# Moving a decay stage under a convolution, and pairing and deferring steps of a 16-chunk loop, in a two-layer hybrid encoder

## The chip, the cores and the metric

The kernel runs on the 8 cores of one Trainium2 chip. Each core computes one element of a batch of 8; nothing is exchanged between cores. The metric is device time in microseconds of the slowest core. Most runs of one kernel agree within 0.3%, but a program on all 8 cores has a second, slower state in some of its runs: one die, or both, shows a lower granted clock and a longer time.

The engines are called as in the profile: PE (matrix), ACT (activation functions), DVE and POOL (vector work), SP (issues transfers). PEld is weight loading on PE.

## The reference, cut to what matters

Two layers; each adds to x the output projection of three branches. The change touches only the state-space (SSD) branch:

```python
def _ssd_branch(u, conv_w, conv_b, a_log, dt_bias, d_skip, norm_w):
    z, xbc, dt = ...                                  # cuts of u
    xbc = silu(_dwconv_centred(xbc, conv_w, conv_b))  # 5 taps
    xs, bm, cm = ...                                  # cuts of xbc
    dt = softplus(dt + dt_bias)                       # two directions x 16 heads
    dta = dt * -exp(a_log)
    y_f = _ssd_chunked(xs * dt[:, :, 0], dta[:, :, 0], bm, cm)
    y_b = flip(_ssd_chunked(flip(xs * dt[:, :, 1]), flip(dta[:, :, 1]), flip(bm), flip(cm)))
    y = y_f + y_b + (d_skip[0] + d_skip[1]) * xs
    y = y * silu(z)                                   # the gate
    return y * rsqrt(mean(y * y, per group) + EPS) * norm_w
```

`_ssd_chunked` works on chunks of 128 positions: it needs the running sum of `dta` within each chunk and, inside a chunk, the products exp(-(difference of running sums)) x scores. With 2048 positions there are 16 chunks; heads come in two groups of 8.

## The kernel before

Each layer does, in the SSD part: a **decay stage** (dt, running sums `cs`, their exponentials, and `cs` transposed and written to memory as `csT_d`); then for each of two groups the convolution, a pass A over the chunk states, and **pass B**, a loop of 16 chunks. Pass B therefore runs four times. `P.op(engine, instruction, reads, writes)` puts an instruction in that engine's queue, in program order; each engine runs its queue in order, and the helper adds the waits that the reads and writes ask for.

The decay stage (cut):

```python
for tt in range(NT):                      # NT = 16
    for k in range(8):
        P.op("pe", MM(ps[0][:, tt*32:(tt+1)*32], c.hdnT[:, k, tt*128:(tt+1)*128], Wdt[:, k, :], ...))
# ... v, softplus on ACT and DVE -> dt, dta
for tt in range(NT):                      # fp32, 16 columns each
    P.op("pe", MM(ps[1][:, tt*32:tt*32+16], c.U, dta[:, tt, 0:16], ...))
    P.op("pe", MM(ps[1][:, tt*32+16:tt*32+32], c.Ur, dta[:, tt, 16:32], ...))
# ... the same with c.onesf (32 columns each), Copies, three Exps, four blocks of transposes
P.op("sp", DMA(c.csT_d..., csT[0:32, :, :]), ...)
P.barrier()
```

Pass B (cut; the short names in the comments are those of the prediction):

```python
def iteration(cn, cc_):                   # cn: the chunk that is prepared, cc_: the one that is finished
    if cn is not None:
        P.op("pe", MM(ps[4], BT[:, tokn], CT[:, tokn]))                   # scores for G
        for k in range(8): P.op("pe", MM(ps[3], c.hdnT[...], Wz[:, k, :]))  # gate
        P.op("dve", TT(Gm[bn][:, 0, :], ps[4], c.U,  ALU.mult))           # G
        P.op("dve", TT(Gm[bn][:, 1, :], ps[4], c.Ur, ALU.mult))           # G
        P.op("dve", TT(Dd, Dd, csv, ALU.subtract))                        # D; Dd is R, loaded from csT_d
        P.op("act", ACT(Dd, Dd, AF.Relu, scale=-1.0))                     # Relu
        P.op("act", ACT(E, Dd, AF.Exp, scale=-1.0))                       # Exp
        P.op("pool", ...)  # three Xt
    if cc_ is not None:
        # PE: Yb = ... from M and Xt;  ps[1], ps[2] from the states
        P.op("dve", TT(ya, ps[1], dout, ALU.mult));  P.op("dve", TT(yb_, ps[2], dout, ALU.mult))
        P.op("pool", TT(ya, ya, yb_, ALU.add))                            # add
        P.op("dve", TT(yy, Yb_, ya, ALU.add))                             # yy
        P.op("pool", TT(yy, yy, sz[b], ALU.mult))                         # gate multiply
    if cn is not None:
        for d in range(2): P.op("dve", TT(Mt[bn][:, d], E[:, d], Gm..., ALU.mult))   # M
        P.op("act", ACT(sz[bn], ps[3], AF.Silu))                          # Silu
    if cc_ is not None:
        P.op("act", Square(yy) -> ssn); P.op("act", Ln); P.op("act", Exp) # 1/rms
        P.op("dve", STT(yo[b], yy, ssn, snw, ALU.mult, ALU.mult))         # yo

def stageC(ci_):                          # transposes of yo on PE, Copy on ACT, then
    P.op("sp", DMA(c.yT[l][...], yst[b]), reads=[t_yst[b]])

for ci_ in range(NT):
    loadS(ci_ + 1); loadR(ci_ + 2)        # on SP: states, and R = a broadcast read of csT_d, 1024 KB
    iteration(ci_ + 1, ci_)
    if ci_ >= 1: stageC(ci_ - 1)
stageC(NT - 1)
```

## Time and profile before

| | before |
|---|---|
| three runs at first, median | 4204.21 us (4198.21 to 4288.53) |
| profiled run, spans of the cores | 4131 to 4155 us |
| median span of each die | 4147.2 and 4143.8 us |
| decay stage, each of two layers | 41.4 us with little beside it |
| from one Relu to the next in pass B | 12.3 us, all four loops |
| Relu of chunk 0 to Relu of chunk 15 | 185.2 us in the first loop, 184.4 to 185.1 in the others |

How to read it: a share of busy time on a page says how full an engine is on average, not what it would be worth to make it faster. Here no engine is over 57% busy, so each stage has to be read by itself: who waits for whom, and which wait ends last. The lines are shown in the prediction.

### The profile page before, as it was taken

Reading aid. Unit: us, or ns where it says so; the run is one execution under the profiler, and the core shown is the slowest. Engines: PE = TensorE matmul, PEld = TensorE weight load, DVE = VectorE, ACT = ScalarE, POOL = GpSimd, SP = SyncE. Lnnn points to the kernel's source line nnn. Section 1 sums busy time; section 2 is a strip of 40 time slices with the busy share of each in tenths; the row PEclk is TensorE's granted clock in tenths of the full one; section 3 lists DMA queues with packets and bytes.
Section 4 is the critical chain, followed back from the end, with each engine's and each line's share of the span. In section 5 each row is a group of like instructions: output and inputs, shape, how many; then the busy total and the mean of one; then the engine's idle time right before and its main releaser. Section 6 shows DMA issues by size and latency. Waiting matters only on the chain.

```text
span 4155.4 us, 54727 instructions; the slowest of 8 cores (4131.4 to 4155.4 us)
## 1 busy us (share of the span) xinstructions
PE 2384.1 (57%) x16712; PEld 1289.3 (31%) x16848; DVE 1841.6 (44%) x3555; ACT 1990.1 (48%) x2949; POOL 671.2 (16%) x592
## 2 busy tenths in 40 slices
PE   1675656775656347343654756566856473473439
PEld 1333333333443114111222333333434341241214
DVE  1553232566605562663113622334766136626631
ACT  4455656454424573573212556564554245644640
POOL 0110000000004451652000100000000025415430
PEclk9988878885567668566887978888955586686669
DMA  5011000031111431344322020000041113522455
GB/s 129 13 16 31 6 5 6 4 60 62 38 35 46 112 110 23 104 122 126 122 66 43 1 44 6 6 5 5 12 96 41 43 33 109 123 27 89 120 138 180
DMA packets 185127, 244.90 MB, mean 59 GB/s; under 512 B 70268, under 2 KB 150140, under 8 KB 182792
## 3 DMA queue, kind: packets, MB, share of 16 engines
q1 hardware_dynamic: 132776, 205.60, 16.3%
q0 software_dynamic: 52064, 35.79, 6.4%
q8 instruction: 142, 2.33, 0.2%
q14 instruction: 145, 1.19, 0.1%
HBM read 226.27 MB, written 50.86 MB: 67 GB/s over the span
## 4 chain that ended last, share of the span: by engine, by line
PE 29%; ACT 22%; DVE 19%; issue 18%; DMA 7%; POOL 4%; DVEq 1%; ACTq 0%; SPq 0%; POOLq 0%
PE psall L233 19%; ACT arena L209 18%; DVE arena L213 10%; PE psall L232 8%; ACT L209 4%; POOL arena L213 3%; DVE arena L227 3%; DVE arena L223 2%; DMA arena<-na_tab 2%; PE psall L237 2%; DVE arena L249 2%; DMA arena<-w_in 1%; DVE arena L218 1%; DVE arena L245 1%; DVEq L173 1%
## 5 line engine op out<-in xcount | busy, mean ns | idle before, releaser
L233 PE MATMUL psall<-arena 128*128 128x512 bf16 (+3 forms) x8144 | 1753.8, 378 | 966.2 <-ACT arena L209 451.2
L209 ACT ACTIVATE arena<-psall 128x1024 bf16<-128x1024 f32 (+5 forms) x1260 | 977.4, 796 | 761.7 <-PE psall L233 476.4
L209 ACT ACTIVATE arena<-arena 128x8 f32<-128x8 f32 (+9 forms) x1232 | 735.4, 604 | 1152.4 <-DVE arena L213 635.5
L233 PEld LDWEIGHTS psall<-arena 128*128 128x128 bf16 (+1 forms) x8280 | 725.5, 110 | 1779.0 <-issue 1300.6
L213 DVE TENSOR_TENSOR arena<-arena 128x512 f32<-128x512 f32 (+7 forms) x1256 | 927.1, 743 | 550.0 <-ACT arena L209 302.4
L232 PE MATMUL psall<-arena 128*128 128x129 bf16 (+4 forms) x7232 | 582.7, 235 | 418.8 <-ACT arena L209 351.6
L213 POOL TENSOR_TENSOR arena<-arena 128x512 bf16<-128x512 f32 (+2 forms) x504 | 616.9, 1237 | 787.4 <-DVE arena L213 729.2
L232 PEld LDWEIGHTS psall<-arena 128*128 128x128 bf16 (+1 forms) x7232 | 469.8, 111 | 628.9 <-issue 624.8
L213 DVE TENSOR_TENSOR arena<-psall,arena 128x512 f32<-128x512 f32 (+1 forms) x466 | 263.7, 577 | 707.9 <-PE psall L233 309.9
L227 DVE COPY arena<-psall 128x512 bf16<-128x512 bf16 (+2 forms) x322 | 160.5, 514 | 508.4 <-PE psall L232 437.5
L237 PE MATMUL psall<-arena 128*128 128x128 bf16 (+1 forms) x1336 | 144.9, 257 | 382.2 <-DVE arena L223 189.7
L223 DVE SCALAR_TENSOR_TENSOR arena<-arena 128x128 f32<-128x128 f32 (+3 forms) x354 | 192.6, 544 | 348.9 <-ACT arena L209 324.7
L209 ACT ACT_TABLE_LOAD x201 | 257.9, 1283 | 97.7 <-PE psall L233 28.5
L241 POOL DMA_DIRECT2D arena<-w_in x46 | 40.7, 885 | 1353.7 <-issue 744.2
L237 PEld LDWEIGHTS psall<-arena 128*128 128x128 bf16 (+1 forms) x1336 | 105.1, 114 | 453.6 <-issue 435.5
L253 POOL MEMSET arena<- 128x2 bf16 (+4 forms) x30 | 7.6, 269 | 1191.2 <-DMA yT<-arena 894.4
L245 DVE TENSOR_REDUCE arena<-arena 128x8 f32<-128x512 f32 (+1 forms) x130 | 82.2, 673 | 31.6 <-ACT arena L209 31.3
L213 DVE TENSOR_TENSOR arena<-arena,psall 128x512 f32<-128x512 f32 x120 | 82.5, 687 | 21.8 <-PE psall L233 17.0
L223 DVE SCALAR_TENSOR_TENSOR arena<-psall,arena 128x64 bf16<-128x64 f32 x256 | 72.5, 283 | 27.5 <-DVE arena L249 0.9
L218 DVE TENSOR_SCALAR arena<-arena 128x128 f32<-128x128 f32 (+1 forms) x138 | 38.4, 279 | 82.6 <-DMA arena<-diff_qk_norm 55.5
L249 DVE RECIPROCAL arena<-arena 128x1 f32<-128x1 f32 x256 | 42.0, 164 | 27.2 <-DVE arena L249 0.7
L209 ACT ACTIVATION_READ_ACCUMULATOR arena<-arena 128x1 f32 x224 | 42.2, 188 | 0.0
(8 smaller groups left out, 68.8 us busy)
## 6 DMA issues: line engine op xcount, KB each, us to landing
arena<-csT_d SPq DMA_DIRECT2D x64, 1024.0 KB, 6.5
arena<-x SPq DMA_DIRECT2D x48, 512.0 KB, 4.6
arena<-na_tab SPq DMA_DIRECT2D x16, 1344.0 KB, 5.9
arena<-w_in POOLq DMA_DIRECT2D x20, 1024.0 KB, 9.6
yT<-arena SPq DMA_DIRECT2D x128, 128.0 KB, 2.0
arena<-yT SPq DMA_DIRECT2D x8, 2048.0 KB, 15.4
arena<-w_out POOLq DMA_DIRECT2D x8, 1024.0 KB, 25.2
sf_d<-arena SPq DMA_DIRECT2D x64, 128.0 KB, 1.7
```

The source lines that it names most:

```text
L173: engobj.wait_ge(sem_of(p), v)
L209: return lambda e: e.activation(out=out, in_=in_, func=func, **kw)
L213: return lambda e: e.tensor_tensor(out=out, in0=in0, in1=in1, op=op)
L218: return lambda e: e.tensor_scalar(out=out, in0=in0, scalar1=s1, scalar2=None, op0=op0)
L223: return lambda e: e.scalar_tensor_tensor(out=out, in0=in0, scalar=scalar, in1=in1, op0=op0, op1=op1)
L227: return lambda e: e.tensor_copy(out=out, in_=in_)
L232: return lambda e: e.matmul(out, lhsT, rhs, start=start, stop=stop, skip_group_check=True)
L233: return lambda e: e.matmul(out, lhsT, rhs, start=start, stop=stop)
L237: return lambda e: e.transpose(out, in_, ident)
L241: return lambda e: e.dma_start(out=out, in_=in_)
L245: return lambda e: e.tensor_reduce(out=out, in_=in_, axis=AX.X, op=(op or ALU.add))
L249: return lambda e: e.reciprocal(out=out, in_=in_)
```

## The change

It has two parts.

1. The decay stage is cut into four pieces that run ahead of chunks 1 to 4 of the convolution of group 0. Its 48 narrow fp32 products become three wide ones.
2. In pass B, Silu for two chunks is done together in every second iteration, so ACT switches tables half as often (the last instruction of the block, an Exp on a constant, brings the exp table back early). The normalisation yo of a chunk moves out of its own iteration to behind ya and yb of the next.

The diff, cut to its core (`...` marks cuts):

```diff
-    for tt in range(NT):
-        P.op("pe", MM(ps[1][:, tt*32:tt*32+16], c.U, dta[:, tt, 0:16], ...))
-        P.op("pe", MM(ps[1][:, tt*32+16:tt*32+32], c.Ur, dta[:, tt, 16:32], ...))
...
+    def make_decay_stages(v, tmp3, csT):
+        def s1():  # dt matmuls into ps[4]; Abs, Exp, Ln
+        def s2():
+            P.op("pe", MM(p5[:, :, 0:16], c.U, dta[:, :, 0:16], skip=True), ...)
+            P.op("pe", MM(p5[:, :, 16:32], c.Ur, dta[:, :, 16:32], skip=True), ...)
+            P.op("pe", MM(ps[6], c.onesf, dta.rearrange("p t h -> p (t h)"), skip=True), ...)
+        def s3():  # three Exps
+        def s4():  # transposes of cs, store to csT_d
+        return [s1, s2, s3, s4]
...
         for n, (kind, ci) in enumerate(chunks):
+            if n >= 1 and stages:
+                stages.pop(0)()
...
-        sz = [A.alloc([128, 512], F32) for _ in range(2)]
+        sz = [A.alloc([128, 512], F32) for _ in range(4)]
+        def silus(cn):
+            if cn is not None:
+                if cn % 2 == 0:
+                    zgate(cn + 1)
+                    for c2 in (cn, cn + 1):
+                        P.op("act", ACT(sz[c2 % 4], zb, AF.Silu), ...)
+                    P.op("act", ACT(ssn[:, 1:2], c.onec, AF.Exp), ...)
...
+                if cc_ >= 1:
+                    normalise(cc_ - 1)
                 P.op("pool", TT(ya, ya, yb_, ALU.add), ...)
...
-                P.op("act", ACT(sz[bn], ps[3], AF.Silu), ...)
...
-                P.op("dve", STT(yo[b], yy, ssn[:, 0:1], ...))
...
             if ci_ >= 1:
                 stageC(ci_ - 1)
+            silus(ci_ + 1 if ci_ + 1 < NT else None)
+        normalise(NT - 1)
```

## The prediction

> **What bounds the kernel now.** I read the cores first (4131 to 4155 us, both dies alike: a fast run), then the page, then three stretches of the timeline of core 0. No engine is near full on the page (PE 57%, ACT 48%, DVE 44%), and the chain that ended last is spread over PE, ACT and DVE, so the change has to be read from the two stages that it touches. Both are in the SSD part, which runs twice (two layers). These lines are from the view of stretches; the fields after the length are busy us of PE, PEld, DVE, ACT and POOL, then clock and DMA:
> ```profile
> 1156.00:1172.60 16.60, 1.79 (x28) 1.79 (x29) 0.52 (x3) 0.23 (x1) 0.89 (x1) 0.50 0.33 90
> 1172.60:1214.00 41.40, 27.80 (x231) 25.37 (x227) 3.52 (x6) 7.08 (x12) 0.00 (x0) 0.54 0.03 7
> 1214.00:1302.40 88.40, 74.42 (x625) 44.96 (x632) 18.24 (x26) 33.49 (x53) 5.58 (x10) 0.95 0.19 19
> 1372.00:1568.00 196.00, 82.40 (x490) 38.63 (x498) 124.03 (x140) 133.62 (x155) 93.84 (x79) 0.67 0.35 104
> ```
> The second stretch is the decay stage (dt, cumulative sums, their exponentials): 41.4 us in which nothing else runs. The third is the convolution of group 0, where PE works 74 of 88 us. The fourth is the loop over 16 chunks (pass B) of one group; four such loops make up some 850 us, and no engine in it is over 70% busy. Its period is 12.29 us, almost without variation, in all four. One period, from the timeline asked for one engine at a time (start, length, group, count, idle time before it and its releaser):
> ```profile
> 1405.15 3.91 ACT L209 ACTIVATE arena<-arena 128x2048 f32<-128x2048 f32 x2 [3.42 <-DVE arena L213]
> 1409.08 1.28 ACT L209 ACT_TABLE_LOAD   x1
> 1410.37 0.60 ACT L209 ACTIVATE arena<-psall 128x512 f32<-128x512 f32 x1
> 1411.65 1.28 ACT L209 ACT_TABLE_LOAD   x1
> 1412.95 0.59 ACT L209 ACTIVATE arena<-arena 128x1 f32<-128x1 f32 x2
> ...
> 1407.77 0.69 DVE L213 TENSOR_TENSOR arena<-psall,arena 128x512 f32<-128x512 f32 x1 [1.51 <-POOL arena L213]
> 1409.23 2.69 DVE L213 TENSOR_TENSOR arena<-arena 128x1024 bf16<-128x1024 bf16 x2 [0.77 <-ACT arena L209]
> 1413.64 0.92 DVE L223 SCALAR_TENSOR_TENSOR arena<-arena 128x512 bf16<-128x512 f32 x1 [1.72 <-ACT arena L209]
> 1414.48 0.67 DVE L213 TENSOR_TENSOR arena<-psall,arena 128x128 bf16<-128x128 f32 x2
> 1415.07 2.28 DVE L213 TENSOR_TENSOR arena<-arena 128x2048 f32<-128x2048 f32 x1
> 1417.27 1.28 DVE L213 TENSOR_TENSOR arena<-psall,arena 128x512 f32<-128x512 f32 x2
> ...
> 1406.40 1.27 POOL L213 TENSOR_TENSOR arena<-arena 128x512 f32<-128x512 f32 x1 [4.69 <-DVE arena L213]
> 1408.66 5.35 POOL L213 TENSOR_TENSOR arena<-arena 128x512 f32<-128x512 f32 x4 [1.00 <-DVE arena L213]
> ```
> Names for what follows: Relu/Exp (the 3.91), Silu, Square, Ln/Exp and Copy on ACT; on DVE the masks G (0.67), the subtraction D (2.28), ya and yb (1.28), the sum yy (0.69), the decay products M (2.69) and the normalisation yo (0.92); on POOL an add between yb and yy, the gate multiply after yy, then three Xt. The loop is one closed ring over ACT and DVE: Relu/Exp to table load 3.93, to Silu 1.29, through Silu and Square to the second load 1.28, load to Ln 1.30, Ln/Exp to yo 0.69, yo and G to D 1.43, D to the next Relu 2.37. Sum 12.29: all of the period. D of the next chunk stands behind yo of this one in DVE's queue, and yo needs the Ln/Exp that stands behind both table loads. That is why neither engine fills.
>
> **What the Trainium skill says.** "ScalarE: Activation LUTs", section "What ACT_TABLE_LOAD costs": 1283 ns a load plus about 1380 ns of drain, 2.66 us a switch. The trace agrees on the load (1.28) and shows no drain (Exp ends at 1409.06, the load starts at 1409.08, Silu at 1410.37), so I use 1.29. Same page, "Table sets": exp and ln share one set; the trace agrees, there is a load only at Silu and at the first function after it. "SBUF — State Buffer", section "Who interferes with whom": DVE and GpSimd share a port pair under an exclusive lock; a DVE instruction with two SBUF inputs and a GpSimd instruction that reads SBUF do not overlap, and whoever comes second waits. The trace agrees. A yo with POOL idle takes 0.75; two that began while POOL worked end 0.55 after POOL's burst, as these show (bursts end at 1389.42 and, above, at 1414.01; yo ends at 1389.97 and 1414.56). The M pair takes 1.49 where POOL is idle and 2.69 beside it:
> ```profile
> 1568.84 0.75 DVE L223 SCALAR_TENSOR_TENSOR arena<-arena 128x512 bf16<-128x512 f32 x1 [3.17 <-ACT arena L209]
> 1384.08 5.34 POOL L213 TENSOR_TENSOR arena<-arena 128x512 f32<-128x512 f32 x4 [1.00 <-DVE arena L213]
> 1388.54 1.43 DVE L223 SCALAR_TENSOR_TENSOR arena<-arena 128x512 bf16<-128x512 f32 x1 [2.39 <-ACT arena L209]
> 1373.12 1.49 DVE L213 TENSOR_TENSOR arena<-arena 128x1024 bf16<-128x1024 bf16 x2 [5.84 <-ACT arena L209]
> ```
> G, ya, yb and yy read PSUM and one SBUF tensor and are free of it.
>
> **The change, part by part.** First, the decay stage goes into the convolution of group 0, as four pieces before chunks 1 to 4. The 41.4 us leave the path. What comes back is PE work, as PE is near its bound there: 128 matmuls of 32 columns, 3.7 us as in the decay stage now; 96 small fp32 passes (20.7 us) become three wide products of 256, 256 and 512 columns. A 128-column fp32 transpose shows 0.25 us at half clock, so a pass costs about 2 cycles a column; two passes over 1024 columns are some 2 us at the 0.95 clock of this stretch (an estimate). Sixteen transposes, 4.0 us at half clock, perhaps 3. Sum 8.7. Their ACT and DVE work (7.1 and 3.5 us) and four more table loads (5.1) lie in slack: ACT is busy 33 of 88 us and four PSUM banks hold 6.9 us of matmuls before PE must wait for a Copy. Gain 41.4 - 8.7 = 32.7 a layer, 65 in all.
>
> Second, pass B. The gate's Silu is done for two chunks at once, so two loads a pair instead of four; yo of chunk c moves behind ya and yb of chunk c+1. The order of the built instructions shows this on DVE: G, D, ya, yb, yo, yy, M. So D no longer waits for ACT, and the ring above is cut. The new ring, from the end of one D (0): ya, yb to 1.20; yo alone 0.75, to 1.87; the POOL add could start at 1.35 but both inputs of yo are in SBUF, so it gets the lock at 1.87 and ends about 3.0; yy 0.1 later, to 3.8; the multiply 0.2 later, to 5.25; M ends 2.0 after the multiply, as now (1409.92 to 1411.92: 0.55, one Xt of 0.9, 0.55), at 7.25; G to 7.85; the second Xt holds the lock to 8.15; D needs 2.2 more: 10.35. So 10.35 instead of 12.29.
>
> ACT beside it: Relu/Exp 0.1 to 4.0, Square after the multiply at 5.35, then Ln/Exp and Copy to 7.3. In every second iteration come load 1.28, two Silus 1.09, load 1.28, dummy Exp 0.3: to 11.25. The next Relu is then 0.8 late and Exp ends at 15.16, but M must wait for the multiply at 15.6 (10.35 + 5.25) anyway. Hidden, by a few tenths. PE: 16 gate matmuls a pair, 3.4 us per chunk at half clock, fit between yo's transposes (2.7) and the next G (7.2).
>
> A loop has 15 intervals. The first stays (9.7). The second, now 15.36 as it holds three loads, becomes about 10: 5.3. Thirteen of 12.32 (mean) become 10.35: 25.6. Sum 31 a loop, 123 for four. With the 65: 188 us of 4204, that is 4016.
>
> **The rivals.**
> (a) ACT becomes the bound: if M does not wait for POOL, the pair is Relu/Exp to the end of the Silu block (about 10.9) plus 9.6, some 10.2 an iteration. Gain 52 x 2.12 = 110, with 21 for the second intervals and 65: 4008. For it: the margin in the ring is 0.3 us. It is almost the same number, so the range covers it.
> (b) No lock trouble and no ACT stall: 9.65 an iteration (D to the multiply 4.86, then 2.0 and 2.79). That is 52 x 2.67 + 21 + 65 = 225, or 3980. Against it: yo and D have two SBUF inputs, and POOL's Xt now run beside D, which it was idle at before.
> (c) The load of R (1024 KB a chunk, 5 to 9 us from issue to landing, median 6.5) becomes the wait: it is issued behind yT's store, at 8.9 after D, and D of two chunks later starts at 18.5. Slack 1 to 4 us with today's landings, but the loop moves 104 GB/s now and some 123 then. If a third of the loads came 2 us late, 52 x 0.7, some 36 us are lost: 4050.
> (d) The PE work in the convolution pushes Copies and Silus late (table loads before chunk 2 and after 3): each delay is under the 6.9 us of banks. If it did cost, 10 us a layer: 4036.
> (e) The gain moves to a wait at group ends, or the clock of PE falls as its work is denser. Nothing in the profile says so: PE is idle more than half of pass B.
>
> **Range and chances.** An iteration between 9.8 and 11.0 moves the total by -29 to +34 us; the front by 10 to either side; runs of one kernel by some 10. I take 3970 to 4070. Reaching less than 2% (above 4120) would need more than half of both parts to fail, or the slow state (4288 was seen) in most runs: 4%. Slower: 1%.
>
> **What would show it.** In the profile after: the interval between two Relus in pass B 10.2 to 10.5 on average; four table loads a layer added in the convolution and half of pass B's gone (201 on the page fall to about 145); M ending 2 us after POOL's multiply; no idle time before D that a csT_d load ends; from the conv_w transposes to the first convolution matmul some 7 us where 48 stand now; the convolution of group 0 about 97 us. I am wrong if Relus keep over 11.5 us apart, if D waits for csT_d or M for ACT, or if the convolution grows by over 20 us.

## The result, and the profile after

| | before | changed |
|---|---|---|
| median of all runs of the comparison | 4198.21 us (15 runs) | 3983.47 us (12 runs) |
| fast runs | 4159 to 4219 us (11 within 1.5% of the fastest, median 4181) | 3973 to 4009 us (8 runs, median 3977) |
| slow runs | up to 4289 us | 4034 to 4116 us (4 runs) |
| median span of each die, profiled run | 4147.2, 4143.8 us | 3964.0, 3961.2 us |
| table loads on ACT | 201 | 145 |
| mean PE clock, dies | 0.754, 0.751 | 0.762, 0.764 |

The ratio of fast runs is 0.9529, with a 95% interval of 0.949 to 0.9568: faster. Here and below a ratio is the mean time of one kernel's fast runs over that of the other's fast runs of the same rounds, so it is not quite the ratio of the medians quoted.

The span fell by 183 us. Two stages account for nearly all of it. The convolution of group 0, from the transposes of conv_w to the first instruction of pass A ("the front" below), took 131.6 us in both layers before, decay stage included; it takes 100.2 and 98.6 (core 0 both times): 64 us. The first pass B, from its first Relu to its last, took 185.19 us and takes 155.25: 29.9 us. The four together took 739.2 us and take 623.1: 116 us, and not four times 29.9, because the other loops had less to lose and the third now has three chunks where D waits for R. Sum 180.

The page's line of engines, after:

```profile
PE 2365.4 (60%) x16668; PEld 1244.5 (31%) x16668; DVE 1846.2 (46%) x3555; ACT 1923.1 (48%) x2925; POOL 796.4 (20%) x592
```

Not much work went away: PE is busy 2365 us instead of 2384, DVE 1846 instead of 1842, ACT 1923 instead of 1990, most of that table loads, which by experiment 5 are not the gain. In pass B the gain is waiting that was closed; in the front it is also some 19 us a layer of narrow products. POOL's 796 us instead of 671 is no more work either, with the same 592 instructions: its instructions now run beside DVE instructions with two SBUF inputs and take longer. The stretches that answer to the four of before (core 2, same columns: busy us of PE, PEld, DVE, ACT and POOL, then clock and DMA):

```profile
1159.00:1175.00 16.00, 1.42 (x12) 1.35 (x12) 0.29 (x2) 0.23 (x1) 0.89 (x1) 0.50 0.34 92
1175.00:1274.00 99.00, 83.47 (x782) 51.41 (x782) 21.83 (x32) 44.66 (x69) 5.78 (x11) 0.94 0.19 20
1347.00:1500.00 153.00, 78.78 (x465) 33.69 (x464) 119.27 (x132) 109.21 (x139) 122.29 (x72) 0.66 0.47 127
```

There are only three: the decay stage of 41 us is gone and its work stands in the second line. In the loop (third line) ACT is busy 71% of the time, DVE 78%, POOL 80% where it was 48% of the stretch before. Next, PE in the front part after the change, asked for on the timeline (core 2; lines in between left out):

```profile
1173.52 1.42 PE L237 MATMUL psall<-arena 6*128 6x6 f32 x12 [18.49 <-issue]
1182.10 9.71 PE L233 MATMUL psall<-arena 128*128 128x512 bf16 x32 [7.16 <-issue]
...
1217.53 1.88 PE L232 MATMUL psall<-arena 128*128 128x256 f32 x6
...
1244.00 1.47 PE L237 MATMUL psall<-arena 128*32 128x128 f32 x12
1246.53 0.60 PE L237 MATMUL psall<-arena 128*32 128x128 f32 x4 [1.05 <-ACT arena L209]
```

and before (core 0; PE, then PEld):

```profile
1181.51 20.66 PE L232 MATMUL psall<-arena 128*128 128x16 f32 x96 [5.66 <-DVE arena L213]
1181.48 20.55 PEld L232 LDWEIGHTS psall<-arena 128*128 128x128 f32 x96 [5.74 <-issue]
```

The same sums that took 96 instructions and 20.66 us take 6 and 1.88 us. The second line shows why: each of the 96 has a weight load of its own, 0.21 us each, and together these fill the whole stretch; the six of the wide products load for 1.27 us. So the narrow products went at the pace of their weight loads, not of their 16 or 32 columns. The transposes take 1.47 + 0.60 instead of four times 1.0, with one wait of 1.05. From the end of the conv_w transposes to the first convolution matmul there are 7.2 us instead of 48.

One iteration of the loop (core 2; DVE, ACT, POOL, each asked for alone):

```profile
1398.83 1.28 DVE L213 TENSOR_TENSOR arena<-psall,arena 128x512 f32<-128x512 f32 x2
1400.03 0.74 DVE L223 SCALAR_TENSOR_TENSOR arena<-arena 128x512 bf16<-128x512 f32 x1
1402.06 0.69 DVE L213 TENSOR_TENSOR arena<-psall,arena 128x512 f32<-128x512 f32 x1 [1.30 <-POOL arena L213]
1403.02 3.20 DVE L213 TENSOR_TENSOR arena<-arena 128x1024 bf16<-128x1024 bf16 x2 [0.26 <-ACT arena L209]
1406.14 0.68 DVE L213 TENSOR_TENSOR arena<-psall,arena 128x128 bf16<-128x128 f32 x2
1406.73 2.54 DVE L213 TENSOR_TENSOR arena<-arena 128x2048 f32<-128x2048 f32 x1
...
1406.33 1.28 ACT L209 ACT_TABLE_LOAD   x1
1407.62 1.08 ACT L209 ACTIVATE arena<-psall 128x512 f32<-128x512 f32 x2
1408.73 1.28 ACT L209 ACT_TABLE_LOAD   x1
...
1400.25 1.64 POOL L213 TENSOR_TENSOR arena<-arena 128x512 f32<-128x512 f32 x1 [0.44 <-DVE arena L213]
1402.96 7.21 POOL L213 TENSOR_TENSOR arena<-arena 128x512 f32<-128x512 f32 x4 [1.07 <-ACT arena L209]
```

The reader can walk the ring: D of this chunk ends at 1398.91; yo (0.74) runs before the add, and although the add is recorded from 1400.25 it cannot end until yo is over: 1.64 instead of 1.27. Then yy at 1402.06 after a wait for POOL, the multiply at 1402.96 (it ends at 1404.22), the two M halves stretched to 3.20 because POOL's work stands between them, G, and D again, which ends at 1409.27. 10.36 us from D to D, and no line in it waits for ACT for more than 0.26 us. (In the iterations between, 1.01 us of idle time before M is put down to ACT, whose Exp ends at 1393.30 in the one before this; but the multiply, which has the lock, runs to 1393.86, so this wait does not hold up the ring.) ACT does two Silus between two table loads in this iteration; the next Relu starts late, and the Relus come 9.60 and 11.13 us apart in turn. D comes every 10.36 all the same.

### The profile page after: what moved, and what is told of

Its sections match the earlier page's. It is cut to its first block, busy times and chain, and to the rows that moved or that the text cites. A ratio compares the mean times of both kernels' runs of the same rounds, so it can differ in the third digit from the quotient of the medians.

```text
span 3972.0 us, 54387 instructions; the slowest of 8 cores (3949.1 to 3972.0 us)
## 1 busy us (share of the span) xinstructions
PE 2365.4 (60%) x16668; PEld 1244.5 (31%) x16668; DVE 1846.2 (46%) x3555; ACT 1923.1 (48%) x2925; POOL 796.4 (20%) x592
## 4 chain that ended last, share of the span: by engine, by line
PE 31%; ACT 21%; DVE 19%; issue 15%; DMA 8%; POOL 4%; DVEq 1%; ACTq 0%; SPq 0%; POOLq 0%
PE psall L233 21%; ACT arena L209 19%; DVE arena L213 10%; PE psall L232 8%; POOL arena L213 4%; DVE arena L227 3%; DVE arena L223 2%; DMA arena<-na_tab 2%; PE psall L237 2%; ACT L209 2%; DVE arena L249 2%; DMA arena<-x 1%; DMA arena<-w_in 1%; DMA arena<-csT_d 1%; DVE arena L218 1%
## 5 line engine op out<-in xcount | busy, mean ns | idle before, releaser
L209 ACT ACTIVATE arena<-psall 128x1024 bf16<-128x1024 f32 (+6 forms) x1260 | 973.4, 795 | 724.4 <-PE psall L233 489.0
L209 ACT ACTIVATE arena<-arena 128x512 f32<-128x512 f32 (+10 forms) x1264 | 739.1, 594 | 1083.7 <-DVE arena L213 490.3
L213 DVE TENSOR_TENSOR arena<-arena 128x512 f32<-128x512 f32 (+7 forms) x1256 | 948.1, 760 | 503.4 <-ACT arena L209 266.2
L233 PEld LDWEIGHTS psall<-arena 128*128 128x128 bf16 (+1 forms) x8280 | 734.5, 111 | 1336.7 <-issue 860.9
L213 POOL TENSOR_TENSOR arena<-arena 128x512 bf16<-128x512 f32 (+2 forms) x504 | 742.2, 1486 | 539.6 <-DVE arena L213 453.6
L232 PE MATMUL psall<-arena 128*128 128x129 bf16 (+4 forms) x7052 | 544.9, 228 | 508.5 <-ACT arena L209 350.8
L232 PEld LDWEIGHTS psall<-arena 128*128 128x128 bf16 x7052 | 415.7, 103 | 721.7 <-issue 718.5
L237 PEld LDWEIGHTS psall<-arena 128*128 128x128 bf16 (+1 forms) x1336 | 105.0, 117 | 664.4 <-issue 656.6
L223 DVE SCALAR_TENSOR_TENSOR arena<-arena 128x128 f32<-128x128 f32 (+3 forms) x354 | 180.4, 510 | 242.8 <-ACT arena L209 217.9
```

The lines of the kernel that those rows point to most:

```text
L209: return lambda e: e.activation(out=out, in_=in_, func=func, **kw)
L213: return lambda e: e.tensor_tensor(out=out, in0=in0, in1=in1, op=op)
L223: return lambda e: e.scalar_tensor_tensor(out=out, in0=in0, scalar=scalar, in1=in1, op0=op0, op1=op1)
L232: return lambda e: e.matmul(out, lhsT, rhs, start=start, stop=stop, skip_group_check=True)
L233: return lambda e: e.matmul(out, lhsT, rhs, start=start, stop=stop)
L237: return lambda e: e.transpose(out, in_, ident)
```

## The experiments

All kernels give correct results. Edits are shown against the changed kernel. The first four ran on one chip, the others on a second; the kernel before ran among them, with fast runs of 4162 to 4169 us on the first and 4162 to 4202 us on the second. "Interval" is the time from one Relu to the next in pass B.

**1. The front part alone** (pass B as before, four of its edits taken back).

```diff
-                if cc_ >= 1:
-                    normalise(cc_ - 1)
...
+                P.op("act", ACT(sz[bn], ps[3], AF.Silu), reads=[tps[3]], writes=[t_sz[bn]])
...
+                P.op("dve", STT(yo[b], yy, ssn[:, 0:1], snw[...], ALU.mult, ALU.mult), ...)
...
-            silus(ci_ + 1 if ci_ + 1 < NT else None)
-        normalise(NT - 1)
```

> Only the decay stage is moved; pass B as before. If the two parts are independent, as I hold: the Relu interval of pass B stays 12.29 us, the front gains 31 us a layer (as in the changed kernel's trace: 131.3 us from the conv_w transposes to the end of the group-0 convolution become 99.9), the total falls by 63 us, ratio to before 0.985. If instead the moved stage only pays because pass B got shorter (or the gain is given back at the next wait), the ratio stays at 1.00.

Measured: ratio 0.9845 (0.9826 to 0.9864), fast runs 4097 to 4102 us. Interval 12.30 us, front 99.9 and 100.8 us. The median span of the cores is 62 us below the kernel before. As expected.

**2. Pass B alone** (the decay stage stands where it stood).

```diff
-            if n >= 1 and stages:
-                stages.pop(0)()
...
+    for tt in range(NT):
+        P.op("pe", MM(ps[1][:, tt*32:tt*32+16], c.U, dta[:, tt, 0:16], ...))
...   # the whole decay stage of the kernel before, back in its place
```

> Only pass B is changed; the decay stage in its old place with its narrow products. Independent parts: Relu intervals alternate 9.60 and 11.13 as in the changed kernel, 120 us saved, ratio 0.971. If the parts share a gain the ratio is above 0.975.

Measured: ratio 0.9727 (0.9705 to 0.9749), fast runs 4050 to 4052 us, median span 114 us down. Intervals 9.60 and 11.13 in turn; a few are longer where D waited 0.2 to 2.2 us for a csT_d load. 62 + 114 = 176 us, against 182 for both parts together (medians of the cores' spans). These longer intervals explain the 6 us that are missing: the four loops take 631 us here and 623 in the profile of the changed kernel. So the two parts add up, within what runs differ by.

**3. Inside pass B: yo deferred, Silu not paired.** Rival to the ring of DVE and POOL: that ACT, relieved of table loads, is what made the loop faster. Then this kernel would lose much.

```diff
-                if cn % 2 == 0:
-                    zgate(cn)
+                zgate(cn)
...
+                P.op("act", ACT(sz[cn % 4], zb, AF.Silu), reads=[t_zb], writes=[t_sz[cn % 4]])   # behind M
...
-            silus(ci_ + 1 if ci_ + 1 < NT else None)
```

> The changed kernel with the Silu done chunk by chunk again (four table loads a pair, two PSUM banks for the gate as in the changed kernel), yo still deferred. My ring theory (D, ya/yb, yo, POOL add, yy, POOL multiply, M, G, D = 10.36 us, ACT is hidden): ACT is done with its last Copy about 9.1 us after D, before D ends again, so every interval is 10.36 with no alternation and the total is that of the changed kernel within 0.3%: ratio 0.953. Rival (table loads and Silu are what the change saved, ACT is the bound): two more loads and the lost batching cost 1.3 us an iteration or more, intervals near 11.7, ratio 0.97 or above.

Measured: two of four runs were fast, 4016 and 4034 us, too few for a ratio; the total expected, that of the changed kernel, was missed: the same ratio as the changed kernel's, 0.9529 of 4165, would be 3969. But the intervals are 10.36, as the ring says, wherever nothing disturbs. 12 of the 60 are 11.5 to 13.6, seven of them in the first loop and none in the third. The trace names the disturber (core 5; SP's queue, then ACT, then DVE):

```profile
1417.80 0.37 SPq L241 DMA_DIRECT2D yT<-arena  x1
...
1419.29 0.38 SPq L241 DMA_DIRECT2D arena<-csT_d  x1
...
1417.07 0.60 ACT L209 ACTIVATE arena<-psall 128x512 bf16<-128x512 bf16 x1
...
1430.01 2.29 DVE L213 TENSOR_TENSOR arena<-arena 128x2048 f32<-128x2048 f32 x1 [3.37 <-DMA arena<-csT_d]
```

ACT's Copy of yo's transposes, behind two table loads of its iteration, ends at 1417.67. The store of yT waits for it on SP, and the load of R for a later chunk stands behind that store in SP's queue: issued at 1419.29, landed only just before D could start at 1430.01, and D had been ready 3.37 us earlier. The Trainium skill, "DMA: Bandwidth & Descriptors", section "Anatomy of one DMA — SWDGE (gpsimd) path", says that any semaphore wait happens on the issuing sequencer before dispatch. The trace agrees: the store holds up three loads that have nothing to do with it. R is issued 10.65 us after D instead of 9.04 in the changed kernel, and so has 7.6 us to land before D is ready, instead of 9.2. In the first loop most landings took 10 to 11 us, in the second 5.8 to 7.8, so not every loop suffers. So the theory of the ring held and the expected total fell, on a cause that needed its own test.

**4. Inside pass B: Silu paired, yo in its old place.**

```diff
-                if cc_ >= 1:
-                    normalise(cc_ - 1)
...
+                normalise(cc_)            # after Square, Ln, Exp, as before the change
```

> The changed kernel with yo back in its old place (after Ln/Exp, ahead of the next G and D), Silu still in pairs. Ring theory with the port lock: M ends 6.9 us after D, yo waits for POOL's second Xt until 7.8 and ends at 8.3, D waits for the third Xt until 9.2 and ends at 11.4: intervals 11.4, 60 us of pass B's 120 are lost, ratio 0.967. Rival (the table loads were the gain): intervals stay near 10.4, ratio 0.953. Without the lock yo would end 7.5 and D 10.4, which looks like the rival, so the position of yo and D against the end of the Xt in the trace decides.

Measured: ratio 0.9698 (0.9628 to 0.9769), three runs at 4027 to 4031 us and one at 4067. Interval 11.37 us without variation. DVE in it (profiled run, core 0, on the die that the lower clock of this run left alone):

```profile
1413.38 1.52 DVE L223 SCALAR_TENSOR_TENSOR arena<-arena 128x512 bf16<-128x512 f32 x1
1414.83 0.68 DVE L213 TENSOR_TENSOR arena<-psall,arena 128x128 bf16<-128x128 f32 x2
```

yo no longer waits for ACT, but it now stands between M and G beside POOL's Xt, and the lock makes it 1.52 us instead of 0.74. So pairing alone is worth 0.93 us a chunk, deferring alone 1.94 where R comes in time, both together again 1.94: they are not two savings but two ways to open the same ring.

**5. Experiment 3 with R loaded earlier**: three chunks ahead, and put into SP's queue ahead of the store.

```diff
+        loadR(2)
         for ci_ in range(NT):
             if ci_ + 1 < NT:
                 loadS(ci_ + 1)
-                if ci_ + 2 < NT:
-                    loadR(ci_ + 2)
             iteration(ci_ + 1 if ci_ + 1 < NT else None, ci_)
+            if ci_ + 3 < NT:
+                loadR(ci_ + 3)
             if ci_ >= 1:
                 stageC(ci_ - 1)
```

> The run with deferral only showed intervals of 10.36 flat on most chunks, but on several D waited 2 to 3 us for a csT_d load that had been issued behind the store of yT, which the two extra table loads had made late. Here the same kernel issues the load of R three chunks ahead, before that store, as soon as Exp has freed the buffer (4.1 us after D instead of about 10). If the late issue is the cause, D waits for no csT_d load inside the loop, all intervals are 10.36, and the total is that of the changed kernel, ratio 0.953 (spans near 3965). If the loads are simply slow because the loop moves more bytes, waits of 1 us and more stay.

Measured: interval 10.36 from the third of each loop on (9.74 and 10.92 to 11.27 before), no D waits for csT_d inside a loop. Two of four runs were fast, 3981 and 3985 us, ratio 0.9539 (0.9463 to 0.9615), the same as the changed kernel within the interval. So the early issue takes the loss of experiment 3 away. It does so even in the fourth loop of the profile, where R mostly took 8.6 to 9.8 us to land, more than the 7.6 that experiment 3 left it. So the loss of experiment 3 came from late issue and slow landings together. And the halving of the table loads is worth, in the changed kernel, no table time at all: what it buys is that SP's queue is held up 1.6 us less.

**6. M as one instruction** of 2048 columns instead of two of 1024, to take POOL's Xt out from between its halves.

```diff
-                for d in range(2):
-                    P.op("dve", TT(Mt[bn][:, d], E[:, d], bc(Gm[bn][:, d, :].unsqueeze(1), ...), ALU.mult), ...)
+                P.op("dve", TT(Mt[bn], E, bc(Gm[bn].unsqueeze(2), [128, 2, 8, 128]), ALU.mult), ...)
```

> The changed kernel with the two decay products M as one instruction of 2048 columns. Lock theory: one lock of 1.1 us right after POOL's multiply replaces 0.55, an Xt of 0.9, 0.55; M ends 6.4 us after D instead of 7.3, D then waits for the first Xt and ends at 9.45. Then ACT with its Silu block becomes the bound in every second iteration: Relu intervals 11.1 and 8.7, mean 9.9 instead of 10.36, some 23 us less in all, ratio 0.947. Without the lock in the ring the mean stays at 10.36. Some D may wait for csT_d, as slack shrinks.

Measured: a miss. Fast runs 3982, 3984 and 4009 us, ratio 0.9538 (0.9463 to 0.9614), no better than the changed kernel. Intervals near the expected 8.7 and 11.1 are there (8.55 and 11.13), but so are 14 of 12.6 to 12.9, and on 25 of 60 chunks D waits 0.2 to 2.2 us for csT_d. The profile fell in the slow state, so its intervals serve only as a hint. In it the two troubles are separate: in the fourth loop no D waits for csT_d, and four intervals are 12.65 to 12.93 all the same. In each of the 14, M (in one of them 1357.55 to 1358.77) had the lock before POOL's gate multiply (1357.84 to 1359.88), and a Silu block follows. The multiply then ends 6.79 us after the Relu instead of 5.22, and the next Relu comes 5.9 us after it in either case, right behind ACT's block. That order was read from the trace, not tested by itself; experiment 12 shows it again, with R out of the way.

**7. A fourth Xt-like multiply on POOL**, into a scratch tile that nothing reads. If POOL had slack (it is busy 80% of the loop) this would cost nothing; by the lock it should cost about half a microsecond a chunk.

```diff
+                P.op("pool", TT(v8(xdum), v8(xs[:, cn, :]), bh(dsum, 8 * g), ALU.mult), reads=[t_xs[cn], t_dsk], writes=[t_xdum])
```

> The changed kernel with a fourth POOL multiply a chunk into a scratch tile that nobody reads; POOL's work grows from 6.6 to some 7.6 us of a 10.36 us period. Lock theory: the fourth runs after D frees the port, yo waits for its end (1.8 after D) and ends at 2.35 instead of 1.86, all behind it moves by 0.5: mean interval 10.85, total up by some 29 us against the changed kernel, ratio 0.960. If POOL's slack is real slack (no lock): 10.36, ratio 0.953.

Measured: ratio 0.961 (0.9552 to 0.9669), fast runs 4011 to 4014 us. Intervals 9.95 and 11.97, mean 10.96 instead of 10.36. yo ends 2.45 to 2.63 us after D (2.35 expected, 1.86 without the fourth multiply). As expected in the mean: POOL's idle time is not slack. Not as expected, D no longer comes evenly, but 9.76 and 12.14 us apart in turn.

**8. The decay stage moved but its products narrow**, to size the two halves of the first part.

```diff
-            P.op("pe", MM(p5[:, :, 0:16], c.U, dta[:, :, 0:16], skip=True), ...)
-            P.op("pe", MM(p5[:, :, 16:32], c.Ur, dta[:, :, 16:32], skip=True), ...)
-            P.op("pe", MM(ps[6], c.onesf, dta.rearrange("p t h -> p (t h)"), skip=True), ...)
+            for tt in range(NT):
+                P.op("pe", MM(p5[:, tt, 0:16], c.U, dta[:, tt, 0:16], skip=True), ...)
+                P.op("pe", MM(p5[:, tt, 16:32], c.Ur, dta[:, tt, 16:32], skip=True), ...)
+            for tt in range(NT):
+                P.op("pe", MM(ps[6][:, tt*32:(tt+1)*32], c.onesf, dta[:, tt, :], skip=True), ...)
```

> The changed kernel with the decay stage moved into the convolution but its fp32 products narrow as before (48 matmuls of 16 or 32 columns, 20.7 us of passes in the old place, instead of three wide ones, 1.9 us in the changed trace). PE is the bound of the convolution, so nearly all of the difference comes back: group 0's convolution 110 us instead of 91, total up by 2 x 18.8 = 38 us, ratio 0.962. If the PE work hides in the convolution's gaps, up by less than 10 us, ratio 0.953 to 0.955.

Measured: ratio 0.9652 (0.9593 to 0.971), fast runs 4016 to 4046 us. The front takes 118.0 and 118.6 us instead of 100.2 and 98.6 (core 0), 38 us in both layers; by the median of the cores it is 34. PE in it (core 4):

```profile
1217.12 17.33 PE L232 MATMUL psall<-arena 128*128 128x16 f32 x96
```

Of the 18 to 20 us a layer, 15.4 are this line against the 1.88 of the wide products. So of the 64 us that the front gained, 34 to 38 are the wide products, once the move is made, and the rest the move.

**9. The changed kernel once more**, as a yardstick on the second chip for the three kernels that follow.

> The changed kernel itself, as the measure for the next three on the same chip and in the same rounds: intervals 9.60 and 11.13, ratio 0.953.

Measured: fast runs 3982 to 4001 us, median 3988, ratio 0.9556 (0.9509 to 0.9603). Here D waits for csT_d in 24 places inside the loops, mostly under 0.9 us, at most 2.8; in the profile of the changed kernel that is shown above there were 4. The median landing time of R is 8.9 us here, 7.3 there, and R has 9.2 us. Two such lines of this run:

```profile
1400.47 2.29 DVE L213 TENSOR_TENSOR arena<-arena 128x2048 f32<-128x2048 f32 x1 [0.30 <-DMA arena<-csT_d]
1411.03 2.29 DVE L213 TENSOR_TENSOR arena<-arena 128x2048 f32<-128x2048 f32 x1 [0.35 <-DMA arena<-csT_d]
```

The changed kernel has used up the time that R has to land. Why R lands later on one run than on another is open.

**10. Deferred yo, unpaired Silu, early R, one M**: experiments 5 and 6 together. With R out of the way, the single M should give what it did not give in 6. Against 6, the pairing is gone too, so only the comparison with 5 isolates M.

```diff
 # the edits of experiment 5, and
+                P.op("dve", TT(Mt[bn], E, bc(Gm[bn].unsqueeze(2), [128, 2, 8, 128]), ALU.mult), ...)
```

> Deferral without pairing, the early load of R, and M as one instruction. In the run with one M alone the loads of R came late and ate the gain; with the early issue they should not. Lock theory: M 1.1 after the multiply, D waits for the first Xt; the second and third Xt then run after D and hold yo until 2.4: multiply ends 5.75 after D, M 6.85, G 7.45, Xt 7.75, D 9.9. Intervals 9.9 flat, some 23 us below the changed kernel, ratio 0.947. If M's split was not in the ring: 10.36, ratio 0.953.

Measured: interval 10.03, flat from the sixth of a loop on, no wait for csT_d inside a loop; fast runs 3955 to 3979 us, median 3964, ratio 0.9504 (0.946 to 0.9547). A loop takes 149.3 us, in experiment 5 it took 155.5. The 0.33 us a chunk are close to expected, and so is the total, 25 us below experiment 9. But the ring closes in another order than expected: from chunk 3 of a loop on, M goes before the gate multiply. M ends 6.75 us after D (6.85 expected), the multiply at 7.88 instead of 5.75, and D then waits for the multiply and not for an Xt. That the sum came out all the same is luck in part.

**11. As 10, with the POOL add moved to DVE**, so that yo and yy no longer go to POOL and back.

```diff
 # the edits of experiment 10, and
-                P.op("pool", TT(ya, ya, yb_, ALU.add), reads=[t_ya, t_yb], writes=[t_ya])
                 P.op("dve", TT(yy, Yb_, ya, ALU.add), reads=[t_Y, t_ya], writes=[t_yy])
+                P.op("dve", TT(yy, yy, yb_, ALU.add), reads=[t_yy, t_yb], writes=[t_yy])
```

> The same, and the add of ya and yb moved from POOL to DVE (yy is made in two DVE steps), which takes POOL's 1.3 us and two hand-overs out of the ring. Multiply ends 5.1 after D, M 6.2, D 9.25, and ACT (Copy ends about 9.2 after D with its four table loads a pair) becomes the bound beside it: intervals 9.3 flat, some 55 us below the changed kernel, ratio 0.940. If DVE's extra 0.7 us a chunk is what counts, it is no faster than the run before.

Measured: fast runs 3918 to 3924 us, median 3922, ratio 0.9396 (0.9353 to 0.9438); intervals mostly 8.8 and 9.6 in turn, mean 9.22 to 9.30 from the third on. As expected in the mean, though not flat (M goes before the multiply in every second iteration, the one of 9.6), and the best kernel: some 66 us below the changed kernel on the same chip (3922 against 3988). A loop of it (core 6; the stretch, then two M of different chunks):

```profile
1340.00:1480.00 140.00, 73.04 (x454) 34.03 (x462) 121.00 (x130) 127.67 (x145) 98.91 (x55) 0.73 0.61 148
```

```profile
1401.12 1.38 DVE L213 TENSOR_TENSOR arena<-arena 128x2048 bf16<-128x2048 bf16 x1 [1.18 <-ACT arena L209]
...
1409.94 1.22 DVE L213 TENSOR_TENSOR arena<-arena 128x2048 bf16<-128x2048 bf16 x1 [0.16 <-ACT arena L209]
```

Now ACT is busy 127.67 of 140 us (91%) and M waits for it. Here, if anywhere, fewer table loads might save time on ACT, which suggests the next run.

**12. As 11, with Silu paired again.**

```diff
 # of the edits of experiment 11, those of zgate and Silu are taken back:
+                if cn % 2 == 0:
+                    zgate(cn)
...
+            silus(ci_ + 1 if ci_ + 1 < NT else None)
```

> The same as the run before, but with the changed kernel's Silu in pairs. ACT's work is then in one lump of 4 us in every second iteration, which the shorter ring no longer hides: pairs of 11.2 and 8.2, mean 9.7, slower than the run without pairing (ratio 0.944 against 0.940). If table loads are what counts, the pairing is faster than without: below 9.3 and below 0.940.

Measured: fast runs 3947 to 4005 us, median 3951, ratio 0.9488 (0.9422 to 0.9554). Slower than 11, as was expected, but by more. Intervals 8.37 and 10.73, ten of 12.3. ACT in one of these (core 4; it begins with Square and ends with the next Relu and Exp):

```profile
1402.87 0.63 ACT L209 ACTIVATE arena<-arena 128x512 f32<-128x512 f32 x1 [2.62 <-POOL arena L213]
...
1407.22 1.28 ACT L209 ACT_TABLE_LOAD   x1
1408.51 4.01 ACT L209 ACTIVATE arena<-arena 128x1 f32<-128x1 f32 x3
```

M had the lock first and ran to 1401.60; the multiply of POOL, beside it, took 2.05 us instead of 1.27 and ended at 1402.72. Square waited for it, and from there to the next Relu ACT has no idle time: Ln/Exp, Copy and the Silu block. D had ended at 1407.05, 1.6 us before that Relu. With a Silu block, the Relu comes 5.9 us after the multiply's end; where M goes first the multiply ends 6.39 us after the last Relu instead of 4.82, and that is all of the difference between 12.3 and 10.73. The ten long intervals are the ten places where M goes first, and no D waits for csT_d here. G, too, waits in 23 places inside the loops, up to 1.74 us, for PE, where the gate matmuls of the odd chunk stand ahead of its scores (in experiment 11 in none); but in the long iteration that wait ends before ACT is free. In experiments 10 and 11 M often goes first as well, and without a Silu block behind it costs no long interval. All this is read from traces only; no run forces the order or moves the gate matmuls by themselves.

## Why the prediction was right, and where its numbers were off

- **The ring of 10.35 us.** Measured 10.36 from D to D. Its parts held too: the multiply ended 5.31 after D (5.25 predicted), M 2.00 after the multiply, at 7.31 (7.25). The interval of Relus alternates because ACT's block makes every second one late: from D to the end of that block 11.31 us (11.25). That it is hidden was right, by 0.6 us: Exp ended at 1414.03, the multiply at 1414.59.
- **The second interval of a loop** fell from 15.36 to 9.91 (about 10 predicted), the first stayed at 9.74, and that loop saved 29.9 us (31). The prediction took the 15.36 for all four loops, but the others had 14.43 to 14.95 before; with the waits for R in the third, four loops saved 116 us (123).
- **The front.** 31.4 and 33.0 us (32.7 each). What came back is 9.1 and 7.0 us of convolution (core 0: 81.9 to 90.9, 82.6 to 89.6), against 8.7. On core 2 the parts are dt matmuls 3.5, wide products 1.88 (the estimate of 2 us), transposes 2.07 and a wait of 1.05, together 8.5. From the end of the conv_w transposes to the convolution 7.2 us (7).
- **Table loads** fell to 145, as predicted. One reading of them was loose: before, the second load of a period stood before Ln, and Square, between Silu and Ln, ran without one.
- **The rivals.** (a) ACT as the bound fell: in the iteration shown it waits 3.05 us for DVE before Relu and 1.46 for POOL before Square, and experiment 5 does without pairing and loses nothing. (b) no lock: fell by the 10.36 and by experiment 7. (c) R: right as a danger, too dark for the changed kernel in its first profile (4 short waits, 1.8 us in all, so the sign "no idle time before D" did not quite hold), but real in experiments 2, 3, 6 and 9. The prediction named the load's slack; it did not see that the pairing is what keeps the issue of R early enough. (d) the convolution pushed late: it grew by no more than the added PE work explains. (e) waits at the starts of the loops are as before (8.37, 3.70, 2.82, 3.16 us before; 8.14, 3.75, 2.73, 3.25 after), and the clock rose.
- **The total** of 4015 was 32 us above the median of 3983, although its sum was nearly right: 188 us against 183 between the two profiled spans. The term that was off is the one that the 188 were taken from. 4204 is the middle of three runs of which one was slow, and lies near the upper end of the kernel's fast runs: the profiled one took 4157 us, the eleven fast ones of the comparison have a median of 4181, and four fast ones on the first chip of the experiments took 4162 to 4169. From 4157 to 4181 the same sum gives 3969 to 3993, and the changed kernel's fast runs have their median at 3977. The ratio says a little more than the spans, 4.71% of 4181 or 197 us; the 14 us between the two are within what runs of the kernel before differ by.

What stays open: why R's landing time differs between runs, and between loops of one run (from chunk 4 on 5.2 to 6.0 us in the first loop of experiment 5, mostly 8.6 to 9.8 in the fourth); and what decides whether M or the gate multiply goes first.

## What to carry to other kernels

Where no engine is full, write the loop down as a ring of waits with durations from the trace, and follow it until it closes on the measured period; the change is worth what it takes out of the ring, and two changes that open the same ring do not add. Look at what shares a queue with a load: a store that waits for a late engine holds back every load behind it. Check the parts of the ring and not only its sum: experiment 10 met its number by another order. And take the base of a prediction from a fast run, not from a median that holds a slow one.

## What the Trainium skill lacked or had wrong

- "ScalarE: Activation LUTs", "What ACT_TABLE_LOAD costs": the load of 1.28 us agrees, but the drain of about 1380 ns that it adds to every switch does not show in this loop. After the change too, a load that begins at 1406.33 is followed by Silu at 1407.62, 0.01 us after its end.
- "SBUF — State Buffer", "Who interferes with whom": the lock is right, and it sets the pace of this loop. The page does not say what happens when one engine has several instructions queued: a waiting DVE instruction gets in between two of POOL's. Two halves of M with one Xt between them took 3.20 us, alone 1.49; M as one instruction took 1.22 where nothing held it. It says that the order of issue decides who blocks, but not that this order can turn round from one iteration of a loop to the next, after which (in traces, not isolated) the multiply of POOL on which the ring hangs takes 2.05 us instead of 1.26.
- "DMA: Bandwidth & Descriptors", "Bandwidth": its 6.15 us for 1 MB is the time in which the DMA engines are busy, measured on transfers that POOL issued; the 6.5 us of R (1024 KB, issued by SP) before run from issue to landing, so the two are near but not the same quantity. No figure there tells how long such a load takes inside a loop: medians of 6.4 to 8.9 us in the kernels here.
- "FP8 and Floating Point Precision", "TensorE Precision Notes": it speaks of four passes for fp32. The trace has two PE instructions for each fp32 product (96 for 48, 6 for 3); how many passes one makes it does not show, so the two need not differ.
- No page gives the cost of an fp32 weight load, which set the pace of the narrow products: 0.21 us for 128x128 in the decay stage before, 0.18 in the convolution (experiment 8), whether 16 or 32 columns follow; 6 instructions that are 256 or 512 columns wide took 1.88 us.
